# Keeping the second span's mixer results in DRAM, moving both projections behind the down product, two recurrence heads at once

## The chip, the cores and the metric

The kernel runs on one core of a Trainium2 chip. The metric is the device time of one execution in microseconds (us), lower is better. A core has a matrix engine (TensorE, PE in the profile; loading its weights is the row PEld), a vector engine (VectorE, DVE), a scalar engine (ScalarE, ACT), GpSimd (POOL), and SyncE (SP), which here issues all transfers. Each engine works through its own list in order; semaphores tie the lists together. DRAM is off the core; SBUF is its working memory and PSUM (eight banks of 128x512 float32) receives what TensorE computes.

## The reference

One layer of a streaming encoder over 2048 tokens of 1024 channels, and a final norm, all in float32:

```python
xn = rms_norm(x, mix_norm_g)
aq, ak, av, mq, mk, mv, mo, ipre, fpre, ga, gm = split(xn @ w_in)
att = chunk_band_attention(aq, ak, av, rel_bias)          # 8 heads, chunk of 64 and 8 before it
hm  = mlstm_chunkwise(silu(conv(mq)), silu(conv(mk)), mv, ipre + b_i, fpre + b_f)   # 4 heads
mlstm_out = sigmoid(mo) * rms_norm(hm, mh_norm_g)
y = sigmoid(ga) * (att @ w_att_proj) + sigmoid(gm) * (mlstm_out @ w_mlstm_proj)
x = x + y @ w_out
x = x + square(relu(rms_norm(x, ffn_norm_g) @ w_up)) @ w_down
out = rms_norm(x, final_norm_g)
```

## The kernel before

The 2048 tokens are four blocks of 512. Blocks 0 and 1 are the first span, blocks 2 and 3 (the "far" blocks) the second. Activations are kept channels by tokens, in tiles of 128 channels by 512 tokens. Every float32 product is made of three faster matmuls: each operand is split into a high and a low part, and high times high, high times low and low times high are added up in one bank (L488 to L490 in `mm3`, L571 in `quad`). So an operand takes a ScalarE cast for the high part and a VectorE subtraction for the low one (`split`, L963 and L968; L965 and L970 where it is scaled), and a weight tile takes the same at L427 and L429. A weight tile of 128x1024 serves 24 matmuls over 512 columns.

The large products (out, up and down) are done over a span with seven block products in place of eight (Strassen's way): an operand set for each of the seven, m = 0 to 6, is made of sums and differences of four tiles. `take_parts` loads the four tiles of a row tile k into five context buffers and makes seven sets of it; sets 0 and 1 are the plain tiles of the first block of the span, sets 2 to 6 need both blocks. `take_y` is `take_parts` for the out product, reading the gated results yp of the projections.

The order on the engines is not that of the program text. The kernel's functions are generators; a planner (`Flow`) steps them on assumed costs, with a priority for each, and emits instructions in the order of its clock, and the frame that builds the program reorders a little more for each engine. Buffers come from pools: 28 split tiles `r` (`rpool`), 16 context tiles `ctx`, 6 temporaries `tmp`, 3 split weight tiles `wsp`, 8 banks. All transfers are issued on SyncE's one queue, in the planned order; a transfer waits for its data and its buffer, and those behind it wait with it. There are 1831 of them, as rows of SyncE's list.

`dense` is TensorE's main thread. For the first span it runs the input products, projections, out, up, and then the down product: seven sets in ORDER = (0, 1, 3, 2, 5, 4, 6), each with four column groups c, 1344 matmuls in all; its operands come from DRAM (`take_u1`, r<-u, a ring of eight tiles). Beside it, the planner lays the heads of blocks 2 and 3 between the down matmuls. There are 8 attention heads for each block (scores L1255, exponentials and division on ScalarE and VectorE up to L1274, transposes of the probabilities in `turn` L1286, weighted sums in `weigh` L1220) and 4 recurrence heads for each block (`rec_head`, L1547 on). `N_REC` recurrence heads are under way at a time; before, one.

The result of these heads, the mixer results, are eight split tiles `B["mix"]` for each block, four of attention and four of recurrence, kept in `rpool`. `project(b)` multiplies them by the two projection weights (192 matmuls for a block), and `merge` gates each result (L789), adds the two (L797) and stores yp. Before, it waits for all eight (`yield "wait", B["mix_ev"]`), and `PROJ = {2: (4,0), 3: (6,2)}` puts the projection of block 2 into the down product's fifth set ahead of its first column group, and that of block 3 into the last set ahead of its third, with 96 down matmuls behind it. The two lines in `down` that do it:

```python
                if PROJ[b][1] == c:
                    yield from self.project(b)
```

After the down product come the second span's out product (`quad` with `after_out`, whose banks are drained at L2015), its up and its down product. `residual` and `final` of the first span run beside them; `final` transposes the finished tiles on TensorE (L2301), after ScalarE has scaled them (L2258).

Of the kernel before, what the change touches and what calls it, by code (L numbers as in the profile page):

```python
# [51 lines left out]
N_REC = 1  # L52
# [4 lines left out]
PROJ = {2: (4,0), 3: (6,2)}  # L57
# [167 lines left out]
class Layer:  # L225
# [99 lines left out]
    def weights(self):  # L325


        part = lambda q, m: ("part", (q, m))
        for b in range(2):
            yield from (("plain", n) for n in range(N_W))  # L330
        for q in range(N_G):
            yield "quad", (q, False)
        yield from (part(q, m) for q in range(N_G, N_G + N_O) for m in range(7))
        for name in IN_ORDER:
            if name[:2] == "vm":
                yield from (part(Q_VM + kk, m) for m in range(7) for kk in range(2))
            else:
                yield "quad", (int(name[2]) if name[:2] == "gm" else Q_IN[name], False)
        for s in range(NS):
            if s == 1:  # L340
                yield from (part(q, m) for q in range(N_G, N_G + N_O) for m in range(7))
            for q in range(N_G + N_O, N_G + N_O + N_F):
                if s == 0 and q >= N_G + N_O + N_USUM:
                    yield "quad", (q, True)
                else:
                    yield from (part(q, m) for m in range(7))
            for p, m in enumerate(ORDER):
                for q in range(N_Q - N_F, N_Q):
                    if s == 0 and (p, (q - N_Q + N_F) / 2) in PROJ.values():
                        yield from (("plain", N_W - 8 + 4 * x + j) for j in range(4) for x in range(2))  # L350
                    yield part(q, m)

# [252 lines left out]
    def down(self, s, m, ring, A, aev, blocks):  # L605
# [4 lines left out]
        for c in range(4):  # L610
            for b in blocks:
                if PROJ[b][1] == c:
                    yield from self.project(b)
# [18 lines left out]
    def dense(self):  # L632
# [80 lines left out]
        for s in range(NS):  # L713
# [26 lines left out]
            for p, m in enumerate(ORDER):  # L740
                if p == 1:
                    fl.spawn(self.residual(s), 2)
                yield from self.down(s, m, ring, *D, [] if s else [b for b in (2, 3) if PROJ[b][0] == p])
            self.banks.want = 0
            O = self.y_operands

    def project(self, b):

        fl, B = self.fl, self.blk[b]
        none = [None] * KT  # L750
# [3 lines left out]
        yield "wait", B["mix_ev"]  # L754
        for j in range(4):
            att = {}
            fl.set(go[j + 1])
            for x in range(2):
                bks = yield from self.pair_tile(B["mix"][4 * x:4 * x + 4], none, "get")
                for n in range(2):  # L760
                    fl.spawn(self.merge(b, x, 2 * j + n, bks[n], gates, att.setdefault(n, [None, Event()])), 1)
        fl.put(self.rpool, *B["mix"])
        if b == 3:
            O = self.y_operands = self.operands()
            for k in range(4):
                fl.spawn(self.take_y(1, k, *O), 2)

    def load_gates(self, b, gates, go):
# [4 lines left out]
        for j in range(0, KT, 2):  # L773
            yield "wait", [go[j // 2]] if j > 0 else self.blk[b]["mix_ev"][:7]
# [231 lines left out]
    def attention_far(self, b):  # L1006
# [7 lines left out]
        for j in range(4):  # L1014
            (B["mix"][j],) = yield "get", self.rpool, 1
# [126 lines left out]
    def head_rest(self, b, h, k, q):  # L1142
# [18 lines left out]
        if B["heads_left"][h // 2] == 0:  # L1161
# [4 lines left out]
            fl.set(B["mix_ev"][h // 2])  # L1166
# [36 lines left out]
    def weigh(self, b, h, u, pieces, slots, pev, done):  # L1203
# [29 lines left out]
        fl.put(self.banks, bk)  # L1233
        r = B["mix"][h // 2]
        cols = slice(u * 256, u * 256 + 256)
# [215 lines left out]
    def recurrence_far(self, b):  # L1451
# [3 lines left out]
        for h in range(MH):  # L1455
            yield "get", self.rec_room, 1
            got = yield "get", self.rpool, 2
            B["mix"][4 + h] = got[1]
            B["ctx"][h] = [got[0].bitcast(F32)[:, 0], got[0].bitcast(F32)[:, 1], None]
            B["ctx"][h] += yield "get", self.ctx, 4  # L1460
# [86 lines left out]
    def rec_head(self, b, h):  # L1547
# [77 lines left out]
        if b > 1:  # L1625
            (og,) = yield "get", self.temp, 1
# [699 lines left out]
    def build(self):  # L2326
# [12 lines left out]
        self.mfar, self.gd = far("mfar", 3 * MH, P, T), far("gate", 2, KT, P, T)  # L2339
        self.ypd = [f32d(f"yp{b}", KT, P, T) for b in range(NB)]  # L2340
# [20 lines left out]
        for b in range(NB):  # L2361
# [3 lines left out]
                gates=Event(), mv_slots=Event(), mv_ev=E(NT), ctx={}, ctx_ev=E(MH), qk_ev=E(2 * MH), og_ev=E(MH),  # L2365
# [92 lines left out]
```

## Time and profile before

| | before |
|---|---|
| median of 3 runs | 2867.71 us (2861.02 to 2868.32) |
| span of the profiled execution | 2865.0 us |
| mean granted TensorE clock | 0.994 |
| mean DMA rate | 211 GB/s, 605.74 MB in all |
| first down matmul of the first span | 1552.70 us |
| first projection matmul of block 2, of block 3 | 1836.18, 2076.32 us |
| first matmul of the second span's out product | 2143.11 us |

The profile is one execution. The page gives busy time by engine and the costliest groups of instructions: line, engine, operation, output and inputs, shape, count, then busy time, mean nanoseconds of one, and the idle time of the engine just before, with what ended it. A stretch gives the same busy times inside a window of the span. The granted clock is the share of full speed that the chip gave TensorE; the busy times of TensorE are modelled ends of pipelined matmuls, so the start of one to the start of the next is the safer measure of what a matmul takes. A wait names the line that waited and the instruction that released it.

### The profile page before, as it was taken

The page shows a single profiled execution, that of the slowest core. Times are in us where ns is not written, and L with a number is a line of the kernel's source. Part 1 is how long each engine was busy: PE and PEld are TensorE (multiplying, and loading weights), DVE is VectorE, ACT ScalarE, POOL GpSimd, SP SyncE. Part 2 cuts the span into 40 slices and gives each one's busy share as a digit, 9 for nine tenths or more (in the row PEclk, how much of TensorE's full clock was granted, in tenths as well). Part 3 has the DMA queues.
Part 4 walks back from the last instruction along what each step waited for, and adds up shares of the span by engine and source line. Part 5 has one row for each costly group of instructions (what it writes and reads, how often), then busy time and mean ns, then how long its engine had stood idle before and what let it go on. Part 6 is the DMA issues. An engine that isn't in the chain of part 4 may idle for free.

```text
span 2865.0 us, 39043 instructions
## 1 busy us (share of the span) xinstructions
PE 2815.4 (98%) x13576; PEld 2350.6 (82%) x13576; DVE 2037.9 (71%) x3783; ACT 1558.1 (54%) x2701; POOL 48.2 (2%) x116
## 2 busy tenths in 40 slices
PE   8999999999999999999999999999999999999998
PEld 7888888888878888877888888788778788888887
DVE  6886479778896867875666887778876744455565
ACT  4664366755444545664556666446644655554444
POOL 0000000000000000000000000000000000000000
PEclk9999999999999999999999999999999999999999
DMA  6327632357765768587878866577567655566563
GB/s 216 100 90 257 240 112 89 129 191 251 255 214 188 250 224 286 179 276 254 305 274 284 256 190 224 185 235 236 188 216 268 216 199 194 189 242 210 188 225 134
DMA packets 276005, 605.74 MB, mean 211 GB/s; under 512 B 30688, under 2 KB 45152, under 8 KB 275808
## 3 DMA queue, kind: packets, MB, share of 16 engines
q1 hardware_dynamic: 275808, 603.26, 62.6%
q8 instruction: 106, 1.74, 0.2%
q14 instruction: 91, 0.75, 0.1%
HBM read 426.98 MB, written 176.16 MB: 211 GB/s over the span
## 4 chain that ended last, share of the span: by engine, by line
PE 83%; DVE 7%; DMA 4%; ACT 3%; issue 1%; POOL 0%; SPq 0%; POOLq 0%; DVEq 0%; ACTq 0%
PE bank L571 36%; PE bank L488 12%; PE bank L489 12%; PE bank L490 12%; PE bank L599 2%; PE bank L1220 2%; PE bank L1255 2%; DMA r<-u 2%; PE bank L1286 1%; DVE wsp L429 1%; DVE r L968 1%; ACT wsp L427 1%; DVE sc L1261 1%; DVE r L1291 1%; DMA x<-ctx 1%
## 5 line engine op out<-in xcount | busy, mean ns | idle before, releaser
L571 PE MATMUL bank<-r,wsp 128*128 128x512 f32 x5208 | 1194.4, 391 | 9.4 <-DVE ctx L1772 7.2
L571 PEld LDWEIGHTS bank<-r,wsp 128*128 128x128 f32 x5208 | 980.0, 189 | 216.5 <-DVE ctx L1772 8.9
L429 DVE TENSOR_TENSOR wsp<-wraw,wsp 128x1024 fp32r<-128x1024 f32 x461 | 563.1, 1222 | 341.5 <-ACT wsp L427 299.0
L427 ACT CAST wsp<-wraw 128x1024 fp32r<-128x1024 f32 x461 | 484.2, 1051 | 493.7 <-PE bank L571 191.6
L488 PE MATMUL bank<-r,wsp 128*128 128x512 f32 x1600 | 640.7, 401 | 0.4 <-DVE ctx L1658 0.3
L490 PE MATMUL bank<-r,wsp 128*128 128x512 f32 x1600 | 625.2, 391 | 0.0
L489 PE MATMUL bank<-r,wsp 128*128 128x512 f32 x1600 | 624.8, 391 | 0.0
L490 PEld LDWEIGHTS bank<-r,wsp 128*128 128x128 f32 x1600 | 300.3, 188 | 64.6
L488 PEld LDWEIGHTS bank<-r,wsp 128*128 128x128 f32 x1600 | 301.1, 188 | 52.4 <-DVE ctx L1658 0.5
L489 PEld LDWEIGHTS bank<-r,wsp 128*128 128x128 f32 x1600 | 301.4, 188 | 51.7 <-DVE r L968 0.2
L1772 DVE TENSOR_TENSOR ctx<-bank,ctx 128x512 f32<-128x512 f32 x174 | 119.0, 687 | 85.2 <-PE bank L571 83.8
L963 ACT CAST r<-r 128x512 fp32r<-128x512 f32 x224 | 136.5, 622 | 78.0 <-DMA r<-u 74.2
L968 DVE TENSOR_TENSOR r<-r 128x512 fp32r<-128x512 f32 x224 | 149.7, 686 | 32.9 <-ACT r L963 31.8
L1270 ACT ACTIVATE sc<-sc,scs 128x640 f32<-128x640 f32 (+4 forms) x128 | 97.4, 761 | 77.1 <-DVE scs L1267 74.7
L1764 ACT COPY ctx<-bank 128x512 f32<-128x512 f32 x174 | 101.1, 582 | 66.7 <-PE bank L571 59.2
L396 DVE TENSOR_TENSOR ctx<-ctx,ctx 128x512 f32<-128x512 f32 x112 | 76.7, 688 | 73.5 <-DMA ctx<-in_wf 56.2
L2131 ACT ACTIVATE ctx<-ctx 128x512 f32<-128x512 f32 x96 | 60.6, 631 | 106.1 <-DVE ctx L1772 106.0
L1261 DVE CUSTOM_DVE_ANT_0 sc<-bank,bias 128x320 f32<-128x320 f32 (+3 forms) x240 | 104.6, 459 | 19.3 <-PE bank L1255 15.6
L1220 PE MATMUL bank<-r,r 128*128 128x256 f32 (+1 forms) x672 | 112.8, 288 | 5.6 <-DVE r L1291 3.6
L1220 PEld LDWEIGHTS bank<-r,r 128*128 128x128 f32 x672 | 100.4, 194 | 19.7 <-DVE r L1291 9.3
L1291 DVE TENSOR_TENSOR r<-bank,r 128x512 fp32r<-128x512 f32 (+1 forms) x168 | 96.9, 594 | 10.7 <-ACT r L1289 9.8
L1289 ACT CAST r<-bank 128x512 fp32r<-128x512 f32 (+1 forms) x168 | 81.8, 516 | 17.4 <-PE bank L1286 13.1
(275 smaller groups left out, 2884.9 us busy)
## 6 DMA issues: line engine op xcount, KB each, us to landing
wraw<-in_wf SPq DMA_DIRECT2D x170, 512.0 KB, 4.2
wraw<-wsum SPq DMA_DIRECT2D x136, 512.0 KB, 3.9
r<-u SPq DMA_DIRECT2D x224, 256.0 KB, 3.8
wraw<-in_w SPq DMA_DIRECT2D x104, 512.0 KB, 3.8
u<-ctx SPq DMA_DIRECT2D x128, 256.0 KB, 2.5
ctx<-in_wf SPq DMA_DIRECT2D x112, 256.0 KB, 4.3
wsum<-ctx SPq DMA_DIRECT2D x112, 256.0 KB, 3.6
u<-tmp SPq DMA_DIRECT2D x96, 256.0 KB, 2.9
```

What stands on the lines that cost most here:

```text
L427: nc.scalar.copy(w[:, 0], raw)
L429: nc.vector.tensor_sub(w[:, 1], raw, w[:, 0].bitcast(F32))
L488: mm(ps, lh, rh, start=first, stop=False)
L489: mm(ps, lh, rl, start=False, stop=False)
L490: mm(ps, ll, rh, start=False, stop=last)
L571: mm(ps, wv[:, x, k, n], a[:, y], start=new and k == 0 and x == y == 0, stop=k == 3 and x == 1, skip_group_check=True)
L963: self.nc.scalar.copy(dst[:, 0], src)
L968: self.nc.vector.tensor_sub(dst[:, 1], src, dst[:, 0].bitcast(F32))
L1220: nc.tensor.matmul(bk[:, c0:c0 + w], st, sl[:, x, o:o + w], start=n == 0, stop=n == total - 1)
L1261: nc.vector.tensor_tensor_reduce(out=e[:, x * w:x * w + w], in0=bks[x][:, :w], in1=br[:, j0 + x * w:j0 + x * w + w], op0=ALU.add, op1=ALU. ...
L1291: nc.vector.tensor_sub(slot[:, 1, :o], bk[:, :o], slot[:, 0, :o].bitcast(F32))
L1772: nc.vector.tensor_add(t[:, o:o + 512], ps, t[:, o:o + 512])
```

## The change

Four things change together. The mixer results of blocks 2 and 3 are no longer split in SBUF when they are made: each piece (64x256 for attention, 128x512 for recurrence) is stored to a new DRAM tensor `mixd` as float32, and `take_mix` loads the tiles back and splits them, starting with the last set of the down product. Both projections stand behind the whole down product, wait for each tile alone (`mix_ev[some]`), and go through their columns in the order 0, 2, 1, 3, with their gates and weights. The operands of the out product are made in two parts: `take_y_low`, behind the projection of block 2, makes sets 0 and 1, and `take_y_rest`, behind that of block 3, makes sets 2 to 6. Two recurrence heads are under way at once; a head holds two context buffers and one temporary where it held four context buffers, keeps its values in the second half of its split tiles, and fills their column of ones on VectorE in place of GpSimd. SyncE's list has 1897 transfers after the change; the number of matmuls is the same.

The diff, without the line that adds `mvh={}` to each block's record:

```diff
@@ -51,3 +51,3 @@
 IN_ORDER = ("gm0", "gm1", "q", "mq", "vm0", "ga0", "k", "vm1", "mk", "ga1", "mo")
-N_REC = 1
+N_REC = 2
 N_USUM = 2
@@ -56,3 +56,2 @@
 EARLY_SUMS.update({i: N_Q - N_F + n for n, i in enumerate((7, 9, 11, 12, 13, 14, 15, 16))})
-PROJ = {2: (4,0), 3: (6,2)}
 
@@ -348,5 +347,6 @@
                 for q in range(N_Q - N_F, N_Q):
-                    if s == 0 and (p, (q - N_Q + N_F) / 2) in PROJ.values():
-                        yield from (("plain", N_W - 8 + 4 * x + j) for j in range(4) for x in range(2))
                     yield part(q, m)
+            if s == 0:
+                for _ in range(2):
+                    yield from (("plain", N_W - 8 + 4 * x + j) for j in (0, 2, 1, 3) for x in range(2))
 
@@ -604,3 +604,3 @@
 
-    def down(self, s, m, ring, A, aev, blocks):
+    def down(self, s, m, ring, A, aev):
 
@@ -610,5 +610,2 @@
         for c in range(4):
-            for b in blocks:
-                if PROJ[b][1] == c:
-                    yield from self.project(b)
             for q in range(2):
@@ -742,5 +739,21 @@
                     fl.spawn(self.residual(s), 2)
-                yield from self.down(s, m, ring, *D, [] if s else [b for b in (2, 3) if PROJ[b][0] == p])
+                if s == 0 and p == len(ORDER) - 1:
+                    O = self.operands()
+                    for b in (2, 3):
+                        fl.spawn(self.take_mix(b), 1)
+                yield from self.down(s, m, ring, *D)
             self.banks.want = 0
-            O = self.y_operands
+            for b in (2, 3) if s == 0 else ():
+                yield from self.project(b)
+                for k in range(4):
+                    fl.spawn((self.take_y_low if b == 2 else self.take_y_rest)(k, *O), 2)
+
+    def take_mix(self, b):
+
+        fl, B = self.fl, self.blk[b]
+        for i in (0, 1, 2, 3, 4, 5, 6, 7):
+            yield "wait", self.mix_kept[b][i]
+            (r,) = yield "get", self.rpool, 1
+            B["mix"][i] = r
+            fl.spawn(self.take_u1(self.mixd[b].ap()[i], r, B["mix_ev"][i]), 1)
 
@@ -749,3 +762,2 @@
         fl, B = self.fl, self.blk[b]
-        none = [None] * KT
         gates = {}
@@ -753,8 +765,8 @@
         fl.spawn(self.load_gates(b, gates, go), 1)
-        yield "wait", B["mix_ev"]
-        for j in range(4):
+        for n, j in enumerate((0, 2, 1, 3)):
             att = {}
-            fl.set(go[j + 1])
+            fl.set(go[n + 1])
             for x in range(2):
-                bks = yield from self.pair_tile(B["mix"][4 * x:4 * x + 4], none, "get")
+                some = slice(4 * x, 4 * x + 4)
+                bks = yield from self.pair_tile(B["mix"][some], B["mix_ev"][some], "get")
                 for n in range(2):
@@ -762,6 +774,2 @@
         fl.put(self.rpool, *B["mix"])
-        if b == 3:
-            O = self.y_operands = self.operands()
-            for k in range(4):
-                fl.spawn(self.take_y(1, k, *O), 2)
 
@@ -772,4 +780,4 @@
                 gates[x, j] = [None, Event()]
-        for j in range(0, KT, 2):
-            yield "wait", [go[j // 2]] if j > 0 else self.blk[b]["mix_ev"][:7]
+        for i, j in enumerate((0, 4, 2, 6)):
+            yield "wait", [go[i]] if i > 0 else self.blk[b]["mix_ev"][:1]
             for x in range(2):
@@ -1014,3 +1022,2 @@
         for j in range(4):
-            (B["mix"][j],) = yield "get", self.rpool, 1
             vo, v = yield "get", self.rpool, 2
@@ -1165,3 +1172,4 @@
                 fl.put(self.rpool, B["vn"][h // 2])
-            fl.set(B["mix_ev"][h // 2])
+            else:
+                fl.set(B["mix_ev"][h // 2])
         fl.set(B["head_done"][h])
@@ -1233,4 +1241,9 @@
         fl.put(self.banks, bk)
-        r = B["mix"][h // 2]
         cols = slice(u * 256, u * 256 + 256)
+        if b > 1:
+            fl.set(done)
+            yield from self.store(self.mixd[b].ap()[h // 2, own, cols], tmp[own, :256],
+                                  self.mix_kept[b][h // 2][h % 2 * 2 + u], self.temp, tmp)
+            return
+        r = B["mix"][h // 2]
         yield "act", act_ns(256)
@@ -1457,5 +1470,6 @@
             got = yield "get", self.rpool, 2
-            B["mix"][4 + h] = got[1]
-            B["ctx"][h] = [got[0].bitcast(F32)[:, 0], got[0].bitcast(F32)[:, 1], None]
-            B["ctx"][h] += yield "get", self.ctx, 4
+            q, k = got[0].bitcast(F32)[:, 0], got[0].bitcast(F32)[:, 1]
+            B["ctx"][h] = [q, k, k]
+            B["ctx"][h] += yield "get", self.ctx, 2
+            B["ctx"][h] += yield "get", self.temp, 1
             B["rec_slots"][h] = got
@@ -1465,3 +1479,4 @@
     def gates_far(self, b):
-        yield "wait", self.blk[b - 1]["mix_ev"][4:] + [self.blk[b]["gf"]]
+        before = self.blk[1]["mix_ev"][4:] if b == 2 else [e[0] for e in self.mix_kept[2][4:]]
+        yield "wait", before + [self.blk[b]["gf"]]
         (bk,) = yield "get", self.banks, 1
@@ -1471,6 +1486,7 @@
         fl, nc, B = self.fl, self.nc, self.blk[b]
-        q, k, mv = (B["ctx"][h][n] for n in (0, 1, 6))
-        mvv = mv.rearrange("p (c n) -> p c n", c=NT)
-        yield "pool", 120
-        nc.gpsimd.memset(mvv[:, :, 128:129], 1.0)
+        q, k = B["ctx"][h][:2]
+        mvr = B["rec_slots"][h][1].rearrange("p a c -> p (a c)")[:, :516].rearrange("p (c n) -> p c n", c=NT)
+        mvv = B["mvh"][h] = mvr.bitcast(F32)
+        yield "dve", 85
+        nc.vector.tensor_copy(mvr[:, :, 128:129], self.ones[:, 0:1].to_broadcast([P, NT]).rearrange("p (c o) -> p c o", o=1))
         for to, x in ((k, MH + h), (q, h)):
@@ -1586,3 +1602,3 @@
             yield "wait", [B["mvh_ev"][h]]
-            mv = [B["ctx"][h][6].rearrange("p (c n) -> p c n", c=NT)[:, c] for c in range(NT)]
+            mv = [B["mvh"][h][:, c] for c in range(NT)]
         (hs,) = yield "get", self.hs, 1
@@ -1625,3 +1641,2 @@
         if b > 1:
-            (og,) = yield "get", self.temp, 1
             yield "wait", [self.m_ev[b, 2 * MH + h]]
@@ -1639,13 +1654,12 @@
         if b > 1:
-            fl.put(self.temp, og)
+            fl.put(self.rpool, *B["rec_slots"][h])
+            fl.put(self.temp, nd)
+            fl.put(self.ctx, w)
+            yield from self.store(self.mixd[b].ap()[4 + h], kt[:, :512], self.mix_kept[b][4 + h][0], self.ctx, kt)
+            fl.put(self.rec_room, 0)
+            return
         yield "wait", [B["kq_all"]]
-        if b < 2:
-            (B["mix"][4 + h],) = yield "get", self.rpool, 1
+        (B["mix"][4 + h],) = yield "get", self.rpool, 1
         yield from self.split(kt[:, :512], B["mix"][4 + h])
-        if b < 2:
-            fl.put(self.ctx, *B["ctx"][h])
-        else:
-            fl.put(self.ctx, *B["ctx"][h][3:])
-            fl.put(self.rpool, B["rec_slots"][h][0])
-            fl.put(self.rec_room, 0)
+        fl.put(self.ctx, *B["ctx"][h])
         fl.set(B["mix_ev"][4 + h])
@@ -1707,2 +1721,35 @@
 
+    def take_y_low(self, k, A, aev):
+
+        fl = self.fl
+        for m, j in ((0, k), (1, 4 + k)):
+            yield "wait", [self.yp_ev[2][j]]
+            (r,) = yield "get", self.rpool, 1
+            A[m][k] = r
+            raw = r[:, 1].bitcast(F32)
+            yield "sp", 900, 2000
+            self.nc.sync.dma_start(raw, self.ypd[2].ap()[j])
+            yield from self.split(raw, r, 0.5)
+            fl.set(aev[m][k])
+
+    def take_y_rest(self, k, A, aev):
+
+        fl, V = self.fl, self.nc.vector
+        got = yield "get", self.ctx, 5
+        a11, a12, a21, a22, s1 = (x[:, :512] for x in got)
+        for b, j, a in ((2, k, a11), (2, 4 + k, a12), (3, k, a21), (3, 4 + k, a22)):
+            yield "wait", [self.yp_ev[b][j]]
+            yield "sp", 900, 2000
+            self.nc.sync.dma_start(a, self.ypd[b].ap()[j])
+        done = []
+        for m, dst, x, y in ((2, s1, a21, a22), (5, a21, a11, a21), (3, a11, s1, a11), (4, a12, a12, a11),
+                             (6, a22, None, None)):
+            if x is not None:
+                yield "dve", dve_ns(512)
+                (V.tensor_add if m == 2 else V.tensor_sub)(dst, x, y)
+            fl.spawn(self.take_split(dst, m, k, A, aev, 0.5), 1)
+            done.append(aev[m][k])
+        yield "wait", done
+        fl.put(self.ctx, *got)
+
     def take_x2(self, s, k, A, aev):
@@ -2339,2 +2386,4 @@
         self.mfar, self.gd = far("mfar", 3 * MH, P, T), far("gate", 2, KT, P, T)
+        self.mixd = far("mix", 8, P, T)
+        self.mix_kept = {b: [E(4 if i < 4 else 1) for i in range(8)] for b in (2, 3)}
         self.ypd = [f32d(f"yp{b}", KT, P, T) for b in range(NB)]
```

More of the change, by code (lines that the diff above doesn't have):

```diff
@@ L1233, in weigh @@
         fl.put(self.banks, bk)
+        cols = slice(u * 256, u * 256 + 256)
+        if b > 1:
[3 more added lines that the diff above has]
+            return
         r = B["mix"][h // 2]
-        cols = slice(u * 256, u * 256 + 256)
         yield "act", act_ns(256)
@@ L2364, in build @@
                 kq_ev=E(AH), q_ev=E(AH), k_ev=E(AH), k_spilt=E(AH), kq_all=Event(), head_done=E(AH),
-                gates=Event(), mv_slots=Event(), mv_ev=E(NT), ctx={}, ctx_ev=E(MH), qk_ev=E(2 * MH), og_ev=E(MH),
+                gates=Event(), mv_slots=Event(), mv_ev=E(NT), ctx={}, mvh={}, ctx_ev=E(MH), qk_ev=E(2 * MH), og_ev=E(MH),
                 mix=[None] * 8, mix_ev=E(8), ga={}, ga_ev=E(8), xs_free=Event(), mid=Event(), vo={}, vn={}, vp_ev=E(4), mvh_ev=E(MH), gf=Event(), rec_slots={}, heads_left=[2] * 4))
```

## The prediction

> **What bounds the kernel now.** I read the page's busy times and costliest groups first, to see which engine sets the span; then stretches of the trace, split at the places where the change cuts, to see where that engine loses time; then the timeline inside the bad stretches.
>
> ```profile
> span 2865.0 us, 39043 instructions
> PE 2815.4 (98%) x13576; PEld 2350.6 (82%) x13576; DVE 2037.9 (71%) x3783; ACT 1558.1 (54%) x2701; POOL 48.2 (2%) x116
> L571 PE MATMUL bank<-r,wsp 128*128 128x512 f32 x5208 | 1194.4, 391 | 9.4 <-DVE ctx L1772 7.2
> ```
>
> TensorE is busy 2815.4 of 2865.0 us, so the change, which leaves the matmuls as they are, can win at most what TensorE idles or spends at a reduced clock near it. The groups with the largest time are matmuls over 512 columns; their idle time is a few microseconds. The stretches (columns: window, length, then busy us and count of each engine; last the granted clock, the DMA share and GB/s) cover the first span's down product, 1552.7 to 2143.1 us, with the heads of blocks 2 and 3 inside it:
>
> ```profile
> core 0: us, PE busy (x) PEld busy (x) DVE busy (x) ACT busy (x) POOL busy (x), PEclk, DMA share, GB/s
> 1552.70:1813.00 260.30, 256.67 (x1411) 219.48 (x1410) 205.22 (x512) 157.40 (x324) 6.71 (x24) 1.00 0.72 224
> 1813.00:1853.00 40.00, 34.69 (x195) 29.98 (x194) 31.51 (x91) 19.16 (x45) 1.30 (x3) 0.91 0.53 164
> 1853.00:2053.00 200.00, 197.37 (x1099) 169.64 (x1098) 165.91 (x401) 116.43 (x242) 5.96 (x14) 1.00 0.70 219
> 2053.00:2093.00 40.00, 34.15 (x175) 28.01 (x174) 27.75 (x61) 19.58 (x46) 1.11 (x2) 0.91 0.62 203
> 1552.70:2143.10 590.40, 572.98 (x3095) 488.58 (x3094) 470.24 (x1120) 335.27 (x689) 15.08 (x43) 0.99 0.69 218
> ```
>
> Two stretches of 40 us stand out. In the first TensorE idles 40.00 − 34.69 = 5.31 us and runs at a mean clock of 0.91, which costs 0.09 × 40 = 3.6 us more: 8.9 us. In the second it is 5.85 + 3.6 = 9.45 us. The two long stretches lose 3.63 + 2.63 = 6.26 us in 460.3 us at full clock, 0.54 us per 40. What happens in the bad ones is in TensorE's timeline (start, length, instruction, idle before it and who ended that):
>
> ```profile
> 1826.18 0.55 PE L1286 MATMUL bank<-const,sc 128*128 128x128 f32 x3 [1.25 <-DVE sc L1274]
> 1829.02 2.40 PE L1286 MATMUL bank<-const,sc 128*128 128x128 f32 x10 [2.29 <-DVE sc L1274]
> 1836.18 0.40 PE L488 MATMUL bank<-r,wsp 128*128 128x512 f32 x1
> ...
> 2063.29 1.37 PE L1286 MATMUL bank<-const,sc 128*128 128x128 f32 x7 [2.87 <-DVE sc L1274]
> 2073.07 0.46 PE L1596 MATMUL bank<-ctx,ctx 128*128 128x129 f32 x2 [1.34 <-ACT r L1237]
> 2076.32 0.50 PE L488 MATMUL bank<-r,wsp 128*128 128x512 f32 x1 [0.31 <-DVE ctx L1658]
> ```
>
> These are the two projections. `project` waits for all eight mixer results of its block, and TensorE works in order, so no down matmul can pass it: the last attention head's softmax (L1274) and transposes (L1286) and the last recurrence head (L1596) run with nothing beside them, until the first projection matmul at 1836.18 and at 2076.32.
>
> **The change, part by part.** *Barriers removed.* Both projections now stand behind the whole down product, and the order of the instructions built from the changed kernel has 126 dense matmuls, 28 us at the 0.227 us below, between the last head's last scores and its last transposes. Each bad stretch falls back to the 0.54 us of its neighbours: 8.9 + 9.45 − 2 × 0.54 = **−17.3 us**. If the last head of block 3 still held TensorE once, half would be left (bound −8.6).
>
> *The final transposes.* The next loss follows right after the down product; a like one lies further on.
>
> ```profile
> 2147.77 0.66 PE L2301 MATMUL bank<-const,ctx 128*128 128x128 f32 x4 [1.69 <-ACT ctx L2258]
> 2143.00:2155.00 12.00, 10.31 (x51) 8.49 (x50) 10.48 (x18) 6.85 (x11) 1.38 (x1) 0.86 0.67 234
> 2223.99 8.23 PE L571 MATMUL bank<-r,wsp 128*128 128x512 f32 x28 [1.91 <-DVE ctx L2015]
> 2222.00:2234.00 12.00, 10.09 (x38) 8.12 (x38) 11.94 (x18) 8.29 (x13) 0.00 (x0) 0.86 0.71 227
> ```
>
> The first costs 1.69 us idle and 0.14 × 12 = 1.7 us of clock, 3.4 us. In the changed order these transposes lie at the end of the down product and in the first projection, with the same producer on ScalarE; I take half: **−1.6 us**, bounds −3.4 and 0. The second (1.91 + 1.7 us) is in the out product, whose drains are the same: nothing.
>
> *The operands of the out product.* Before, `take_y` built seven operand sets behind the last projection, while the last 96 down matmuls ran. Now sets 0 and 1 come from block 2 alone and are ready early, but sets 2 to 6 need the last results of block 3 and nothing is left to run except sets 0 and 1. I count VectorE's list in the changed order from the end T0 of the last projection matmul, with these durations:
>
> ```profile
> 2133.72 0.68 DVE L1741 TENSOR_TENSOR ctx<-ctx,ctx 128x512 f32<-128x512 f32 x1
> 2134.32 1.29 DVE L970 SCALAR_TENSOR_TENSOR r<-ctx,r 128x512 fp32r<-128x512 f32 x2
> 2135.53 1.22 DVE L429 TENSOR_TENSOR wsp<-wraw,wsp 128x1024 fp32r<-128x1024 f32 x1
> 2136.66 0.68 DVE L970 SCALAR_TENSOR_TENSOR r<-ctx,r 128x512 fp32r<-128x512 f32 x1
> 2137.27 0.68 DVE L2197 TENSOR_TENSOR ctx<-bank,ctx 128x512 f32<-128x512 f32 x1
> 2163.59 12.27 PE bank L571 x54
> ```
>
> Start to start, a 512-wide operation takes 0.60 us, a weight split 1.13 us; a matmul takes 12.27 / 54 = 0.227 us. The last operand of set 3 (its fourth row tile) is the 41st instruction of that list: 38 of 0.60 us and 3 weight splits give 22.8 + 3.4 = 26.2 us, and about 1 us of waits for banks and ScalarE's halves makes **T0 + 27**. TensorE has in front of it, in its changed order, sets 0 to 3 and the first matmuls of set 5: 99 matmuls, of which the last four need that operand. Undelayed they end at 99 × 0.227 = T0 + 22.5; now at 27 + 4 × 0.227 = 27.9. Loss **5.4 us**, in pieces of up to some 1.8 us (the second row tile's neighbours wait at T0 + 14, 18, 21.5 and 24, since each row tile costs VectorE 10 × 0.60 us). A piece of 1.69 us was enough above for 1.7 us of clock, so I add one such spell: **+7.1 us**. Bounds: without it and with the 1 us of waits gone, 26.2 + 0.9 − 22.5 = 4.6; if TensorE followed the plain order (set 2 to its end, then set 3), the third and fourth row tiles of set 2, ready at about T0 + 18.4 and T0 + 24.4, hold it for 4.8 and 4.6 us with two spells, 12.8.
>
> [...]
>
> *The loads behind it* are off the path:
>
> ```profile
> yp<-tmp SPq DMA_DIRECT2D x16, 256.0 KB, 3.3
> ctx<-yp SPq DMA_DIRECT2D x24, 256.0 KB, 3.9
> u<-ctx SPq DMA_DIRECT2D x128, 256.0 KB, 2.5
> r<-u SPq DMA_DIRECT2D x224, 256.0 KB, 3.8
> ```
>
> The last result of block 3 is merged about 2 us after T0, stored (3.3) and read back (3.9): near T0 + 9, or T0 + 13.5 where SyncE's order puts it behind a weight load that waits for its buffer. VectorE reaches its use after T0 + 20. The 40 stores of mixer results and 16 reloads add 66 transfers net of others to 1831 and some 10 MB. The reload of the last attention tile (store 3.3 by the row, load 3.9, split 1.3, together 8.5 us) has over 150 matmuls of 0.227 us, 34 us, in front of it.
>
> *A denser head stage.* Sixteen attention heads (eight per block) and eight recurrence heads had 1344 + 384 = 1728 dense matmuls as cover, now 1344. What VectorE did for the projections leaves the stage:
>
> ```profile
> L429 DVE TENSOR_TENSOR wsp<-wraw,wsp 128x1024 fp32r<-128x1024 f32 x100 | 122.0, 1220 | 21.8 <-ACT wsp L427 20.5 <-PE bank L2301 0.6 <-DMA r<-u 0.2
> L789 DVE SCALAR_TENSOR_TENSOR tmp<-tmp,bank 128x512 f32<-128x512 f32 x32 | 21.9, 685 | 19.4 <-PE bank L490 19.4
> L797 DVE TENSOR_TENSOR tmp<-tmp,tmp 128x512 f32<-128x512 f32 x16 | 11.0, 688 | 0.3
> ```
>
> 16 weight splits of 1.22, 21.9 and 11.0 make 52.4 us. The stage was 470.24 / 590.4 = 80% busy on VectorE; it becomes (470.24 − 52.4) / (590.4 − 17.3 − 384 × 0.227) = 417.8 / 485.9 = 86%. Its free share falls from 20 to 14%, and if the small stalls grow as its inverse, 6.26 / 460.3 = 1.36% of 485.9 us, 6.6 us, becomes 9.4: **+2.9 us**. Bounds 0 (the reloads' splits are full 512-wide, 16 operations in place of 32 narrow ones, and a second recurrence head gives the planner something to put beside a waiting softmax) and +9 (the stalls more than double). VectorE's eight small copies of ones in place of POOL's fills lie inside this.
>
> Sum: −17.3 − 1.6 + 7.1 + 2.9 = **−8.9 us**. The profiled span of 2865.0 us becomes 2856.1; it lies 2.7 us under the median of the three runs (2861.02 to 2868.32), 0.7 under their mean 2865.7, and I name **2857 us**. All the good ends together give −17.3 − 3.4 + 4.6 + 0 = −16.1, all the bad ones −8.6 + 0 + 12.8 + 9 = +13.2.
>
> **The rivals.** *The gain comes whole.* The out product's operands come in time because TensorE waits elsewhere first or VectorE is ahead: no 7.1, density nothing: −18.9, 2847 us. For it: the list has waits that the count puts in. Against: VectorE's 41 operations have no slack.
>
> *The gain is given back in the out product.* Plain order and two clock spells: 12.8 and density 4: −17.3 − 1.6 + 12.8 + 4 = −2, 2864 us. For it: at 2223.99 the same product already waits for VectorE. Against: the changed order interleaves sets 2 and 3.
>
> *A barrier stays.* The last mixer tile, through DRAM, still makes the second projection wait: half of the first term returns, −8.9 + 8.7 = −0.2, 2866 us. Against: the 34 us of cover.
>
> *Slower: SyncE's queue in the head stage.* All transfers are issued in order by SyncE, and now 40 stores, each waiting for a head's VectorE result, stand before the down product's operand loads.
>
> ```profile
> SPq L2115 <- PE bank L489: 39.4, 56, 2.0
> SPq L2165 <- DVE r L1239: 9.5, 4, 5.7
> 1580.84 5.85 DMA r<-u
> ```
>
> Operand loads are issued the moment their slot comes free (L2115, 56 waits), and one load is seen on the chain that ended last; a transfer held by an attention result waited 9.5 / 4 = 2.4 us. If the 40 stores pass a quarter of that, 0.6 us each, to TensorE, it is +24: −8.9 + 24 = +15, 2881 us. It decides from 8.9 / 40 = 0.22 us per store. Against: SyncE waits much already while TensorE idles only 6.26 us in 460.
>
> **How the numbers follow.** Chances: forecast 0.45, whole gain 0.17, given back 0.16, barrier stays 0.05, slower 0.17. A measurement here tells 0.3%, 8.6 us, from no change: faster means under 2859.1. The forecast's own range, 2851 to 2863, lies two thirds below that: 0.33, with the whole gain 0.50 for faster. Same: 0.12 + 0.14 + 0.04 = 0.30. Slower: 0.17 and a little of the two middle rivals, 0.20. The range runs from 2845, under the whole gain, to 2877, between the bad ends (2866 + 11 of the 13.2) and the slower rival's 2881; beyond it lie about 2 in 10.
>
> **What would show it.** Barriers: no stretch with a clock under 0.95 before the projections, and no idle over 1.5 us at L1286. Operands: in the first two sets' wake, waits of the out product for VectorE's splits, in sum 4 to 8 us, none over 2.5. Density: DVE near 86% up to the projections, small stalls near 9 us. Slower rival: waits for r<-u and a longer down product. The prediction is wrong if the stretch from the first down matmul to the first out matmul is not 15 to 20 us shorter after allowing for the stalls of density.

## The result and the profile after

| | before | changed |
|---|---|---|
| median of 6 runs | 2864.99 us (2861.02 to 2868.32) | 2857.86 us (2854.16 to 2859.91) |
| span of the profiled execution | 2865.0 us | 2855.5 us |
| first down matmul, first out matmul of the second span | 1552.70, 2143.11 us | 1548.82, 2130.23 us |
| between the two | 590.41 us | 581.41 us |
| from there to the end | 721.89 us | 725.27 us |

The ratio is 0.9973 (95% interval 0.9961 to 0.9985): 7.7 us less by the ratio, 4 to 11 by its interval. The page of the changed kernel, its span, busy times and costliest group, as before:

```profile
span 2855.5 us, 39050 instructions
PE 2807.1 (98%) x13576; PEld 2342.3 (82%) x13576; DVE 2027.8 (71%) x3765; ACT 1550.2 (54%) x2679; POOL 47.8 (2%) x108
L571 PE MATMUL bank<-r,wsp 128*128 128x512 f32 x5208 | 1193.5, 390 | 15.1 <-DVE ctx L1819 8.4
```

The idle time ahead of the L571 matmuls rose from 9.4 to 15.1 us: that is where something was given back. The stretches of the changed kernel, from its first down matmul: the whole way to the out product, the head stage, the rest with the projections, and the first 40 us of the out product.

```profile
1548.82:2130.23 581.41, 570.92 (x3143) 488.76 (x3142) 449.93 (x1085) 325.13 (x661) 16.74 (x38) 1.00 0.76 241
1548.82:2005.00 456.18, 446.56 (x2544) 384.33 (x2543) 374.33 (x983) 278.46 (x598) 12.96 (x36) 1.00 0.75 233
2005.00:2130.23 125.23, 124.36 (x601) 104.42 (x600) 75.60 (x103) 46.67 (x63) 3.78 (x2) 1.00 0.79 269
2130.23:2170.23 40.00, 33.30 (x130) 24.36 (x129) 36.50 (x55) 20.21 (x30) 0.00 (x0) 0.96 0.79 257
```

The two bad stretches are gone: up to the out product TensorE idles 10.5 us where it idled 17.4, and its clock is whole where it lost 3.4 us in each (6.83 us at half clock, a granted 0.50, from 1828.22 and from 2063.74 us; the 3.6 in the prediction comes from the rounded 0.91). The out product's first 40 us now idle 6.7 us. TensorE's timeline there, with the out product starting at 2130.23:

```profile
2142.95 3.00 PE L571 MATMUL bank<-r,wsp 128*128 128x512 f32 x12 [1.68 <-DVE ctx L2062]
2146.45 2.49 PE L571 MATMUL bank<-r,wsp 128*128 128x512 f32 x8 [0.50 <-ACT r L973]
2150.65 4.09 PE L571 MATMUL bank<-r,wsp 128*128 128x512 f32 x10 [1.71 <-DVE ctx L2062]
2154.92 0.73 PE L571 MATMUL bank<-r,wsp 128*128 128x512 f32 x2 [0.18 <-ACT r L973]
2156.06 1.20 PE L571 MATMUL bank<-r,wsp 128*128 128x512 f32 x4 [0.41 <-DVE r L978]
2158.04 1.92 PE L571 MATMUL bank<-r,wsp 128*128 128x512 f32 x6 [0.78 <-ACT r L973]
2161.31 3.02 PE L571 MATMUL bank<-r,wsp 128*128 128x512 f32 x12 [1.35 <-ACT r L973]
...
2252.22 2.02 PE L571 MATMUL bank<-r,wsp 128*128 128x512 f32 x7 [1.86 <-DVE ctx L1819]
```

The seven waits up to 2161 us make 6.61 us. Two of them, 3.39 us, name bank drains (L2062) and the others operand splits (L978, and their casts L973), but the drains and the splits stand in one VectorE list, which is busy 36.50 of the 40 us. The wait at 2252.22 is one of the up product's drains; it takes the place of the one at 2223.99 before.

Not all of the profiles' difference of 9.5 us belongs to the change. Up to 1528 us TensorE, VectorE and ScalarE have the same instruction order in both kernels, TensorE up to 1543 us, and yet 3.9 us lie ahead of the first down matmul; most of it between 1200 and 1400 us (before, then changed):

```profile
1200.00:1400.00 200.00, 192.81 (x835) 158.12 (x834) 136.15 (x177) 115.29 (x175) 0.00 (x0) 0.98 0.78 269
```

```profile
1200.00:1400.00 200.00, 193.51 (x849) 158.60 (x848) 138.30 (x179) 116.75 (x178) 0.00 (x0) 1.00 0.80 273
```

There the kernel before idles 0.7 us more and has a clock of 0.98, 6.83 us at half clock from 1309.39 or a loss of 3.4: the same instructions waited otherwise in that execution. The change itself made 5.6 us between these two profiles, 7.1 between the medians.

### The profile page after: what moved, and what is told of

Read it like the earlier page. It is cut to its first block, busy times and chain, and to the rows that moved or that the text cites. A ratio compares the mean times of both kernels' runs of the same rounds, so it can differ in the third digit from the quotient of the medians.

```text
span 2855.5 us, 39050 instructions
## 1 busy us (share of the span) xinstructions
PE 2807.1 (98%) x13576; PEld 2342.3 (82%) x13576; DVE 2027.8 (71%) x3765; ACT 1550.2 (54%) x2679; POOL 47.8 (2%) x108
## 4 chain that ended last, share of the span: by engine, by line
PE 82%; DVE 7%; DMA 5%; ACT 3%; issue 2%; POOL 0%; SPq 0%; POOLq 0%; DVEq 0%; ACTq 0%
PE bank L571 35%; PE bank L488 12%; PE bank L489 12%; PE bank L490 12%; PE bank L599 2%; PE bank L1228 2%; PE bank L1268 2%; DMA r<-u 2%; PE bank L1299 2%; DVE wsp L429 1%; DMA ctx<-in_wf 1%; DVE r L976 1%; DMA wsum<-ctx 1%; ACT wsp L427 1%; DMA sc<-x 0%
## 5 line engine op out<-in xcount | busy, mean ns | idle before, releaser
L571 PE MATMUL bank<-r,wsp 128*128 128x512 f32 x5208 | 1193.5, 390 | 15.1 <-DVE ctx L1819 8.4
L571 PEld LDWEIGHTS bank<-r,wsp 128*128 128x128 f32 x5208 | 977.2, 188 | 225.8 <-DVE ctx L1819 8.6
L971 ACT CAST r<-r 128x512 fp32r<-128x512 f32 x240 | 146.2, 622 | 88.1 <-DMA r<-u 75.4
L976 DVE TENSOR_TENSOR r<-r 128x512 fp32r<-128x512 f32 x240 | 161.1, 688 | 41.6 <-ACT r L971 40.2
L1268 PE MATMUL bank<-r,r 128*128 128x320 f32 (+3 forms) x480 | 88.1, 309 | 1.8 <-DVE ctx L1652 0.9
```

What stands on the lines that cost most here:

```text
L571: mm(ps, wv[:, x, k, n], a[:, y], start=new and k == 0 and x == y == 0, stop=k == 3 and x == 1, skip_group_check=True)
L971: self.nc.scalar.copy(dst[:, 0], src)
L976: self.nc.vector.tensor_sub(dst[:, 1], src, dst[:, 0].bitcast(F32))
L1268: nc.tensor.matmul(bks[x][:, :w], q[:, y, i * P:(i + 1) * P], kf[:, f * P + x * w:f * P + x * w + w], start=y == 0, stop=y == 1)
```

## The experiments

Twelve kernels were run, each beside the kernel before, whose median was 2863 to 2866 us in each group; kernels of different groups are better compared by their ratios. Each has one profile, and the way from the first down to the first out matmul can differ by 6 us between two profiles with the same TensorE order (f0 and i2 below). "Head matmuls" below are those that belong to heads; where many stand between two down or projection matmuls, nothing covers their waits.

### One recurrence head at a time

```diff
-N_REC = 2
+N_REC = 1
```

> The changed kernel with N_REC back at 1, all else kept. If the gain comes from the two barriers (both projections behind the whole down product), one recurrence head at a time costs little: 0 to +3 us against the changed kernel (2858 us), and no clock dip before the projections. Rival: the gain comes from the second recurrence head, since the last recurrence head is what the projections waited for at the end of each barrier; then +8 us or more, with a wait at L488 or at the recurrence's matmuls ahead of the projections.

2856.36 us, ratio 0.9974 (0.9964 to 0.9984): the same as the changed kernel. No clock dip anywhere from 1540 to 2260 us (a granted 1.00 in every 2 us), in a profile that is the fastest of its eleven executions (2846.45 us). On the changed kernel the second recurrence head was worth nothing that shows.

### The final transposes behind their scale: a base for others

With the projections inside the down product, and four banks held by it, the first span's final transposes can take the other four banks while the scale that they wait for needs one. One line rules that out; f0 is this line alone.

```diff
 def final_out(...):
-        yield "wait", scaled
+        yield "wait", scaled + ([ready] if s == 0 else [])
         (bk,) = yield "get", self.banks, 1
```

> The changed kernel with one line more: the first span's final transposes take their bank after the scale of their rows is ready. It is the base for e2 and e4. Both theories: within 2 us of the changed kernel.

2849.81 us, ratio 0.9952 (0.9939 to 0.9965). Missed: 8 us better than the changed kernel by the medians, 6 by the ratios, whose intervals just touch. From the first down to the first out matmul it takes 578.0 us with 6.9 us idle. All 64 final transposes of the first span stand ahead of the out product, as in the changed kernel; before, half of them stood behind its start. The profiles differ by 7.3 us: 2.7 of these lie between the first down matmul and 2001 us, where TensorE's order is the same in both, and 5.4 behind the out product's start. How the line comes to those is open. On the kernel before, the same line is worth little:

> The kernel before with the one line of f0 (final transposes take their bank after the scale). It can only take away the stall of 3.4 us at the transposes: 2861 to 2865 us, and both barriers stay with their half clock. Rival: the line itself is worth the 8 us that lie between the changed kernel and f0; then 2857 us or less.

2864.59 us, ratio 0.9988 (0.9977 to 0.9999), as the first alternative said; both barriers stay. Comparisons below that go by f0 or h2 have the line on both sides.

### The old places, with results through DRAM

```diff
+PROJ = {2: (4, 0), 3: (6, 2)}
 # down(): at these places
+                if PROJ[b][1] == c:
+                    yield from self.project(b)
 # project(): ahead of the first column
+                yield "wait", B["mix_ev"]
 # take_mix of block 2 is started with the fourth set, of block 3 with the sixth
```

> The projections back at their old places inside the down product (fifth set, and ahead of the third column group of the last), each waiting for all its eight tiles, with results through DRAM and two recurrence heads kept; operand sets as in the changed kernel, built behind the second projection; final transposes wait as in f0. If place and wait for all make the barriers, the two stretches with a half clock come back: +17 us of loss there, less the operand stalls of about 8 that 96 down matmuls cover: +8 to +10 us against f0. Rival: the barriers came from one recurrence head at a time, or from the late splits in SBUF; then they stay away and the kernel is within 2 us of f0 or faster.

2852.36 us, ratio 0.9955 (0.9943 to 0.9967), 2.6 us from f0. The stretches around the two projections, whose first matmuls are at 1835.82 and 2061.53 us:

```profile
1820.00:1860.00 40.00, 38.44 (x227) 32.59 (x226) 33.52 (x86) 20.40 (x45) 0.59 (x4) 1.00 0.56 182
2060.00:2100.00 40.00, 39.80 (x180) 32.70 (x178) 24.45 (x32) 13.04 (x18) 0.00 (x0) 1.00 0.92 311
```

The projections wait for all their tiles at the old places, and the barriers do not come back: 1.6 us idle at the first, 0.2 at the second, whole clock. The rival holds, 0.6 us outside its 2 us. The out product of e4, from 2126.98 us, waits for no operand and no drain in its first 40 us, with 96 down matmuls behind the last projection. It still loses 3.7 us of idle time and 3.4 of clock (a granted 0.50 from 2134 to 2140 us) to two waits for final transposes, the longer one here:

```profile
2134.20 0.90 PE L2353 MATMUL bank<-const,ctx 128*128 128x128 f32 x3 [2.16 <-ACT ctx L2310]
```

Next, the same with one recurrence head (and block 3's projection one column group later):

> As e4 (results through DRAM, projections at old places, each waiting for all its tiles) but with one recurrence head at a time, and block 3's projection ahead of the last column group of the last set instead of the third. If the results' way through DRAM is what took the barriers away (buffers of the mixer results no longer hold back block 3's heads), it stays near e4, 2850 to 2856 us, without a half clock before the out product. If the second recurrence head took them away, a stall with a half clock comes back near the first projection: 2860 us or more.

2854.01 us, ratio 0.9964 (0.9951 to 0.9976), inside the first alternative's 2850 to 2856. Its other half is not clean: around the first projection a part of the loss is back.

```profile
1800.00:1840.00 40.00, 35.29 (x189) 29.88 (x187) 35.33 (x108) 21.38 (x43) 0.62 (x4) 0.96 0.63 193
2060.00:2100.00 40.00, 39.45 (x193) 32.88 (x193) 19.15 (x25) 13.89 (x17) 1.01 (x1) 1.00 0.78 264
```

4.7 us idle and 1.7 of clock at the first, against 8.9 in the kernel before; 0.6 at the second. A lone wait of 2.02 us of the last recurrence heads, with a half clock (0.96 over 1990 to 2030 us), stands between. So the way through DRAM takes away the second barrier without the second recurrence head, and the first in part; by these two profiles the second recurrence head takes most of the rest there. Both kernels also keep the smaller set of buffers of a recurrence head that came with the change; it was not tried by itself, nor was a second recurrence head with results in SBUF.

### Later places, with results in SBUF

```diff
 # the kernel before with the line of f0
-PROJ = {2: (4,0), 3: (6,2)}
+PROJ = {2: (5,0), 3: (6,3)}
```

> h2 with both projections further back, ahead of the first column group of the sixth set and the last of the seventh (results still split in SBUF, one recurrence head). If place makes the barriers, they shrink: 5 us or more faster than h2. If the results' buffers make them (block 3's heads wait for slots until the first projection has run), the barriers only move and grow, as block 3's heads have less left to hide in: 5 us or more slower than h2.

2872.24 us, ratio 1.0025 (1.0015 to 1.0036): 7.6 us slower than h2. Place alone does not take the loss away: from the first down to the first out matmul h4 needs 591.7 us with 19.6 idle, h2 590.1 with 19.2. No wait over half a microsecond stands ahead of its first projection, and the second barrier has grown. Two stretches that overlap, around the second projection:

```profile
2040.00:2080.00 40.00, 33.85 (x223) 28.78 (x222) 33.52 (x110) 25.69 (x67) 2.24 (x4) 1.00 0.43 135
2060.00:2100.00 40.00, 32.81 (x201) 27.16 (x202) 30.84 (x87) 21.85 (x63) 2.01 (x2) 1.00 0.31 94
```

Most of what h4 loses against h2 lies behind that: its out product, with 48 down matmuls fewer ahead of it, idles 7.2 us in its first 40 against 1.0, and takes 402.0 us together with the up product against 392.7.

TensorE's orders tell how the barriers move. Listed are the largest clusters of head matmuls in the traces, after so many matmuls of down product and projections:

```
before     89 at 768, 62 at 1440
changed    none over 24
e4         44 at 768, 64 at 780
h4         178 at 1488
```

With the results in split tiles, block 3's heads come late whatever the place; later projections leave more of them at the end. A cluster is not a loss by itself: the two of e4 run with the 1.6 us idle shown above. That the 28 tiles are what they wait for follows from the code and from e4, and was not tried by itself.

### More stores

Each mixer result is stored a second time, to a tensor that is never read: with a place in the planner (e6), or right beside the first store (e6b), with TensorE's order unchanged.

```diff
+            yield from self.store(self.mixe[b].ap()[4 + h], kt[:, :512], Event())   # e6
             yield from self.store(self.mixd[b].ap()[4 + h], kt[:, :512], ...)

+        if twin is not None:                          # e6b, inside store()
+            self.nc.sync.dma_start(twin, src)
         self.nc.sync.dma_start(dst, src)
```

> The changed kernel with every mixer result stored twice, the second time to a tensor that nobody reads: 40 transfers and 5 MB more in SyncE's queue of the head stage. If the queue is not a limit there, 0 to +3 us against the changed kernel. If each store costs TensorE 0.2 us or more (the slower rival of the prediction), +8 us or more, in waits for operand loads (r<-u) during the heads.

> As e6 (each mixer result stored twice), but the second store is issued right beside the first, without a place of its own in the planner, so TensorE's order is that of the changed kernel instruction for instruction. If e6's +12 us came from the stores on SyncE's queue, they come again: +8 us or more against the changed kernel (2858 us). If they came from the other order that the planner made of it, 0 to +2 us.

e6: 2870.19 us, ratio 1.0011 (1.0003 to 1.0020), 12 us over the changed kernel by the medians, 11 by the ratios. e6b: 2861.25 us, ratio 0.9993 (0.9981 to 1.0004), 3.4 over it by the medians and 5.7 by the ratios, whose intervals touch: between the two expectations. So the 40 transfers themselves cost 0.09 to 0.14 us each, if anything, and the rest of e6's loss is the order that the planner made around them. The stretch from the first down to the first out matmul, e6 and then e6b:

```profile
1548.60:2141.03 592.43, 576.28 (x3143) 490.85 (x3142) 449.50 (x1085) 322.56 (x660) 14.72 (x38) 0.99 0.77 242
```

```profile
1551.46:2135.46 584.00, 573.65 (x3144) 489.77 (x3143) 449.75 (x1085) 326.37 (x661) 15.61 (x38) 1.00 0.77 247
```

16.2 us idle in the one, 10.4 in the other, as in the changed kernel (10.5).

### The operands of the out product

Cover (e2): both projections one column group earlier, with f0's line, so that 48 down matmuls follow them. Order (i2): f0 with VectorE's splits for sets 5, 4 and 6, and the difference for set 4, behind the work for 2 and 3. Both (i3).

```diff
 # e2, in down(), last set
+            if O is not None and c == 3:
+                yield from self.both(O)      # both projections, and take_y_low, take_y_rest
 # i2, in take_y_rest
-            fl.spawn(self.take_split(dst, m, k, A, aev, 0.5), 1)
+            if m != 5:
+                fl.spawn(self.take_split(dst, m, k, A, aev, 0.5), 1)
+        fl.spawn(self.take_y_late(k, got, A, aev), 4)     # split 5, then 4 and 6
```

> Both projections stand ahead of the last column group of the last down set, so 48 down matmuls (10.9 us) run behind the second projection, while VectorE builds operand sets 2 to 6; the first span's final transposes also wait for their scale (as in f0). If the out product's new stalls (6.4 us idle and 1.7 us of clock in the changed kernel) come from operands that are late for want of cover, they go: -6 to -8 us against f0, waits of L571 in the first 40 us under 1.5 us. Rival: the transfers are the limit (DMA share 0.87 to 0.93 there); then the stalls stay within 2 us of what they were.

> f0 with VectorE's work for the out product's operands ordered by need: sums and splits of sets 2 and 3 first for each row tile, those of sets 5, 4 and 6 behind. If the stall comes from the order of VectorE's list, the waits of the out product in its first 40 us fall by 2 us or more and the kernel by as much. If the late data of the last two row tiles set it, within 1 us of f0.

> e2 (48 down matmuls behind the second projection) and i2 (operand work by need) together, on f0's line. If the operands of the out product are then in time, its idle time in the first 40 us falls under 1.5 us, without half clock, and the kernel is 2846 us or less, unless a later wait of the out product takes the gain as in e2 (2850 us); then that wait is at a bank drain (the line of the wait on VectorE's drain in the second half of the out product).

e2: 2850.01 us (ratio 0.9947, 0.9936 to 0.9959). Its out product idles 1.9 us in 40 against 4.8 in f0, yet the kernel is no faster than f0: a wait of 2.80 us for a drain, with another half clock that costs 1.7 us (a granted 0.50 from 2208 to 2210 us), comes 80 us later. i2: 2849.86 us (0.9955, 0.9943 to 0.9968), like f0; in the out product's first 60 us it idles 4.2 us against f0's 4.8, in shorter pieces and without a half clock (a granted 1.00, where f0 has 0.50 from 2146 to 2150 us). Its TensorE order is that of f0, instruction for instruction, and VectorE's is the same up to 2125 us; yet from the first down to the first out matmul it took 583.6 us with a half clock (0.72 from 1796 to 1802 us), f0 578.0. That is how far one profile can stray. i3: 2856.47 us (0.9968, 0.9956 to 0.9979), slower than either, though the intervals touch. Its one long wait, SyncE's queue before it (start, length, transfer), and the stretch of that time, with the out product starting at 2125.62:

```profile
2159.20 3.22 PE L571 MATMUL bank<-r,wsp 128*128 128x512 f32 x6 [7.49 <-ACT r L977]
```

```profile
2143.40 0.38 SPq L1747 DMA_DIRECT2D ctx<-yp  x1
2144.72 0.33 SPq L409 DMA_DIRECT2D wraw<-in_wf  x1
2145.15 0.92 SPq L2376 DMA_DIRECT2D out_x<-tmp  x2
2146.16 0.44 SPq L2060 DMA_DIRECT2D ctx<-in_xt  x1
2146.64 2.07 SPq L2376 DMA_DIRECT2D out_x<-tmp  x2
2148.76 2.77 SPq L2060 DMA_DIRECT2D ctx<-in_xt  x4
2151.81 0.91 SPq L1747 DMA_DIRECT2D ctx<-yp  x2
```

```profile
2144.00:2158.00 14.00, 7.71 (x39) 6.17 (x36) 1.56 (x3) 1.87 (x4) 0.00 (x0) 0.93 0.99 353
```

The last two operand loads (L1747) stand behind ten other transfers: a weight load, four stores of results (L2376) and five loads of x (L2060). So they leave 26 us after the out product's start, 8 us behind the load before them. The transfer engines are full in that stretch (0.99, 353 GB/s); ScalarE and VectorE do almost nothing, and ScalarE's cast waited 12.09 us for the load. One more kernel has a long wait at this place, f0 with one recurrence head:

> f0 with one recurrence head at a time. If the second recurrence head is worth something, it is slower than f0 (2850 us) by 3 us or more; if, as e1 and h1 suggest, it is worth nothing, within 2 us of f0.

2857.25 us, ratio 0.9975 (0.9965 to 0.9984), 7.4 us over f0, with one long wait:

```profile
2146.68 8.43 PE L571 MATMUL bank<-r,wsp 128*128 128x512 f32 x27 [5.41 <-ACT r L973]
```

The casts ahead of that one had waited 3.09 us for a VectorE difference and 0.83 us for an operand load; and the profile is the slowest of its ten executions (2863.77 us). By the medians the second recurrence head is worth 7 us on f0 and nothing on the changed kernel. That it does so by the turn that the operand loads get is not shown.

Of the versions run, f0, e2 and i2 are the fastest (2850 us). The intervals of f0 and i2 touch that of the changed kernel, that of e2 ends just under it (0.9959 and 0.9961), and the three do not differ among each other.

## Why the prediction was right, and where not

The time was forecast at 2857 us and is 2857.86; a sum of −8.9 us stands against −7.1 between the medians. That they lie so close is in part luck, since two profiles of one order differ by more (f0 and i2), and since one term has the wrong reason. By the last of its own signs the prediction fails: the stretch from the first down to the first out matmul is 9.0 us shorter, 12 after allowing for the 2.9 of density, not 15 to 20. The step that it left out is work that moved into the stretch, some 4 us of final transposes; with them it is 16. The terms, by the profiles:

- *Barriers, −17.3.* Right in size: the two clusters with their half clocks are gone, and idle time and clock to the out product fell from 17.4 + 6.8 to 10.5 us, which is 13.8, with the denser stage's stalls inside (17.3 − 2.9 = 14.4 by the sum). Wrong in its reason. The step "both projections now stand behind the whole down product" was given as the cause; e4 has them at the old places without barriers, h4 has them later and idles as long up to the out product as h2 does (19.6 and 19.2 us). What removed them was the results' way through DRAM with the buffers that it frees, with the second recurrence head helping at the first projection (h1); by the code it no longer ties block 3's heads to block 2's projection. The prediction had no rival of that kind. Its size held because the prediction read from the built order of the changed kernel that the barriers go, and the order shows that whatever the reason.
- *Final transposes, −1.6.* The stall of 3.4 us after the down product is gone; 0.87 us is left of it in the projections, so nearer −2.5. The transposes themselves moved with it, about 32 of 0.1 us and eight smaller matmuls, some 4 us of work into the earlier stretch. That is most of why the stretch fell by 9.0 and not by 13.8.
- *Operands, +7.1.* Measured 6.6 to 6.7 us idle and 1.7 of clock: 8.4. Half of the idle time, 3.4 us, is waits for bank drains, which the prediction took to be the same as before; only 3.2 are waits for operands. The count of VectorE's list was right in kind; its last operand was forecast for 27 us after the last projection matmul, and the last wait ends at 31, since VectorE waited 1.1 us for a load of x and ScalarE's casts came late. That the loads are off the path was right for this kernel and only just: in i3 they set the wait. With 96 down matmuls of cover (e4) no wait for an operand or a drain is left in the first 40 us.
- *Density, +2.9, from small stalls of 9.4 us.* Measured 456.18 − 446.56 = 9.6 us. VectorE's share is 374.33 / 456.18 = 82% there and 81% up to the first projection, not 86%, so the agreement of the stalls rests less on that formula than it looks.
- *Left at nothing:* the drain wait at 2223.99 vanished, and the one at 2252.22 came (1.86 us and 1.7 of clock): zero in sum. From the out product to the end idle time rose by 5.5 us and lost clock by 1.0, the moved work took some 4 away, and the stretch is 3.4 us longer; about 1 us stays open.
- *The slower rival* had too high a price: 0.09 to 0.14 us for each extra store (e6b), hardly clear of the noise, where 0.22 would have decided. e6 shows the other way to the same loss, an order around the stores that the prediction did not price.

## What to carry to other kernels

When a wait for "all results" stalls an engine, ask first what the late results themselves wait for; moving the wait further back can leave more of them at the end, while a place in DRAM, which frees their buffers, let them run ahead here. Count the cover that a moved piece of work takes along: the operand work behind the last projection lost its 96 matmuls and cost some 8 us of the 17 that the barriers had taken. With one in-order queue for all transfers, an urgent load is behind all that was put ahead of it (ten transfers and 8 us in i3), and a planner that sees small differences will shuffle several microseconds that no single edit owns.

## What the runs showed of the hardware

In these runs the length of an idle spell does not tell by itself whether half clock follows. In the changed kernel 1.93 us that ended at 1798.10 left the clock whole, while after 1.71 us that ended at 2150.65 it was halved for a time:

```profile
1798.10 0.44 PE L1299 MATMUL bank<-const,sc 128*128 128x128 f32 x2 [1.93 <-DVE tmp L1240]
```

```profile
1796.00:1802.00 6.00, 4.07 (x21) 3.35 (x21) 3.92 (x11) 3.58 (x9) 0.00 (x0) 1.00 0.75 190
2150.00:2156.00 6.00, 4.82 (x12) 2.96 (x12) 6.00 (x11) 1.82 (x3) 0.00 (x0) 0.72 0.91 294
```

In 6 us at 0.72 lie 1.7 us; the clock is a granted 0.50 from 2151.32 to 2154.73. After the 1.86 us that ended at 2252.22 it is 0.50 from 2253.72 to 2257.13. At the L1299 matmuls of the first row i2 idled 2.91 us, up to 1797.57, and its clock from 1796 to 1802 us is 0.72. What decides between the two is not shown.
